# All eight u tiles of a hybrid encoder layer in seven products, with pairs of u and gates in turn

## The chip, the cores and the metric

The kernel runs on one core of a Trainium2 chip. The core has five engines with queues of their own: PE (TensorE, matmuls), DVE (VectorE), ACT (ScalarE), POOL (GpSimd) and SP (SyncE, which here issues the loads of weights). The metric is the device time of one execution in microseconds (us). The profile stores times in us from the start of the span unless marked ns.

## The reference

One layer of an encoder over 512 positions of width 1024, in float32. Cut to what matters here:

```python
x1 = x  + rmsnorm(W_out(sig(a_ret) * W_ret_o(Retention(h)) + sig(a_sgu) * W_sgu_o(SGU(h)))),  h = rmsnorm(x)
y  = x1 + rmsnorm(ConvGatedMLP(rmsnorm(x1)))

q, k, v, g, u, sv, a_ret, a_sgu = split(h @ w_in)       # 512, 512, then six of 1024 columns
y_ret = (layernorm(retention(q, k, v)) * silu(g)) @ w_ret_o
sv    = layernorm(gelu(sv)) in chunks of 128 positions, 4 groups of 256 columns
mixed = einsum('gpq,bnqgc->bnpgc', w_spatial, sv) + b_spatial
y_sgu = (gelu(u) * mixed) @ w_sgu_o
```

The change concerns u, the gate sig(a_ret), the output of the retention branch W_ret_o, and `mixed`.

## The kernel before, in words

Activations lie transposed: a tile has 128 features by 512 positions, and eight tiles make 1024 features. Every float32 operand is split into a high and a low part of the rounded type fp32r, and a product is three matmuls: high by high, high by low, low by high. A split is a copy on ACT (the high part, L97) and a subtraction on DVE (the low part, L116).

There are two ways to make output tiles. A *whole* tile (`f_block`) takes one weight block of 128x1024 and 8 x 3 = 24 matmuls of 512 columns. A *Pair* makes two output tiles at once, in seven products of half the width in place of eight (Strassen's way): 7 x 12 = 84 matmuls of 256 columns, with seven weight forms, four of which are sums (`w_form`, T1 to T4), and with ready sums of the activations. For the pairs of gates (`GATE0` to `UP0`) T2 and T4 are summed on POOL (L201, L204), for others on DVE. A Pair holds three PSUM banks, numbered 0 to 2, and has three parts:

- the first part: product into bank 0, which ACT copies to SBUF; product into bank 1, which DVE adds to it; product into bank 2; a fourth one that goes on adding in bank 0, behind the first copy, and is copied by ACT too
- the second: product with S3, again into bank 0, copied by ACT, and subtracted by DVE from bank 2
- the third: one more product into bank 0, behind that copy, and one into bank 2; DVE scales them by the row norm `rbc`, and ACT applies gelu or sigmoid.

The stage in question comes after the retention's own work and ends before the gates of the SGU branch. In order on PE, before: four whole u tiles (`UW = 4`), two u Pairs, then four times `gated_pair(ogh, ogl)`: a Pair of gates with two whole tiles of the retention's output between its parts (of which DVE multiplies the PSUM result by the gate, L1051), followed by two mixes `mix(2 * j)`, `mix(2 * j + 1)`, 16 small matmuls over positions, after which DVE forms mix and multiplies u by it and the result yh, yl is split for the SGU branch's product. The statistics and the norm of sv (`sv_stats`, `sv_scale`, `sv_norm`; L717 on ACT) hang behind the u tiles. After the stage four `gated_pair(yh, yl)` follow.

What sets the order: the code is recorded operation by operation, and a scheduler places the instructions of every engine in a queue; `tc.issue_after(x)` forces what follows behind x. Weights are asked for LOOK = 4 units ahead of use in the order of the list `units` (L111 on), are loaded by SP into four tiles `raw` (128x1024, 512 KB), split into nine slots, and wait there. A queue works off its instructions strictly in order, so a row that waits holds the rows behind it.

Of the kernel before, what the change touches and what calls it, by code (L numbers as in the profile page):

```python
# [15 lines left out]
P = 128  # L16
# [9 lines left out]
EPS = 1e-6  # L26
NW = 146
SV0, U0, GATE0, GATE1 = 24, 32, 40, 72
UW = 4
LOOK = 4  # L30
NBLK = 66
WARM = 17
# [17 lines left out]
def tile_block(ctx: ExitStack, tc, xT, x, wall, par, cs, wsp, bsp, gpost, gffn, out):  # L50
# [48 lines left out]
    def two(t):  # L99
        return t.rearrange("p (n c) -> p n c", n=2)  # L100
# [176 lines left out]
    def w_get(look=LOOK):  # L277
# [9 lines left out]
            n += w_size(u)  # L287
        return w_ready.pop(i)

    def mm3(o, ah, al, bh, bl, start, stop, skip=False):  # L290
        nc.tensor.matmul(o, ah, bh, start=start, stop=False, skip_group_check=skip)  # L291
        nc.tensor.matmul(o, ah, bl, start=False, stop=False, skip_group_check=skip)  # L292
        nc.tensor.matmul(o, al, bh, start=False, stop=stop, skip_group_check=skip)  # L293


    part = const("part", [P, NPAR])
# [603 lines left out]
    class Pair:  # L900
# [9 lines left out]
        def product(self, b, act, first, w=None):  # L910
            wh, wl = w or w_get()
            o = self.b[b][:, T0]
            for k in range(4):
                c = slice(k * P, (k + 1) * P)
                h_, l_ = act(k)
                for n, (w_, a_) in enumerate(((wh, h_), (wh, l_), (wl, h_))):
                    self.last = nc.tensor.matmul(  # L917
                        o, w_[:, c], a_, start=first and k == n == 0, stop=k == 3 and n == 2,
                        skip_group_check=True,
                    )  # L920
            return self.two(o)

        def x(self, first, t):
# [46 lines left out]

    bst = lo64("bst", F32)
    nc.gpsimd.dma_start(bst, bsp.rearrange("g p -> (g p)")[None, :].to_broadcast([P, S]))
    uT, late = [], None
    U_HOMES = [lambda: lo64("u", F32), lambda: hi192("u", F32)] + [lambda: blk(n="u")] * 2 + [lambda: hi192("u", F32)] * 4
    for j in range(UW):
        with tc.issue_after(summed) if j == 0 else ExitStack():
            o = f_block(xh, xl, KD)
        u = U_HOMES.pop()()
        i = v.tensor_mul(two(u), in_turn(o), two(rbc)).ins
        g = nc.scalar.activation(out=u, in_=u, func=AF.Gelu_apprx_tanh).ins  # L980
        uT.append(u)
        with tc.issue_after(i):
            sv_stats(((0, 1), (2, 3), (), ())[j])
        if j == 1:
            sv_scale()
        if j > 1:
            with tc.issue_after(g):
                sv_norm(j - 2, range((NT, 2)[j - 2]))
    for j in range(UW // 2, KD // 2):
        p = Pair(AF.Gelu_apprx_tanh, lambda: U_HOMES.pop()(), None, rbc)  # L990
        p.part1()
        if late:
            late.part3()
        p.part2()
        late = p
        uT += p.t
        if j == UW // 2:
            with tc.issue_after(p.copied):
                sv_norm(1, range(2, NT))
    yh, yl = [], []  # L1000

    def mix(j):
        gs = slice((j // 2) * P, (j // 2 + 1) * P)
        add = tmp("add", (P, P))
        v.scalar_tensor_tensor(
            out=add, in0=rws[:, gs], scalar=col(LNB + j), in1=bst[:, gs],
            op0=ALU.mult, op1=ALU.add,
        )
        o = ps()
        for t in range(NT):  # L1010
            nc.tensor.matmul(  # L1011
                o[:, t * P : (t + 1) * P],
                svz[t, j // 4][:, (j % 4) * P : (j % 4 + 1) * P],
                wst[:, gs],
                start=True,
                stop=True,
            )
        m = tmp("mix")
        v.scalar_tensor_tensor(
            out=m.rearrange("p (t q) -> p t q", t=NT),  # L1020
            in0=o.rearrange("p (t q) -> p t q", t=NT),
            scalar=col(LNG + j),
            in1=add[:, None, :].to_broadcast([P, NT, P]),
            op0=ALU.mult,
            op1=ALU.add,
        )
        v.tensor_mul(uT[j], m, uT[j])
# [6 lines left out]
    def gated_pair(ah, al, late=None):  # L1034

        p = Pair(AF.Sigmoid, lambda: tmp("sig"), None, rbc)
        with tc.issue_after(late.last.ins) if late else ExitStack():
            p.part1()
        if late:
            with tc.issue_after(p.last.ins):  # L1040
                late.part3()
# [5 lines left out]
    r = []  # L1047
    for j in range(KD // 2):
        for o, t in gated_pair(ogh, ogl, late if j == 0 else None):
            b = (lo64("r", F32) if j == 0 else hi192("r", F32) if j < 3 else blk(n="r"))  # L1050
            v.tensor_mul(two(b), in_turn(o), two(t))  # L1051
            r.append(b)
# [608 lines left out]
```

## Time and profile before

| | |
|---|---|
| median of three runs | 785.31 us (785.3 to 785.34) |
| profiled execution | 785.08 us |
| its span | 783.3 us |
| PE busy | 775.6 us, 99% |
| DVE busy | 626.5 us, 80% |
| ACT busy | 467.8 us, 60% |
| POOL busy | 104.0 us, 13% |
| granted clock of PE | 0.998 |

The span is what the profiler recorded from the first to the last instruction; the execution's time is 1.78 us more. Rows of a group give the line, the engine, the operation, output <- input by name, and times; the chain that ended last is followed back from the last instruction, at each step to what released it.

### The profile page before, as it was taken

The numbers are of one execution on the slowest core, as the hardware profiler recorded it, in microseconds if no ns is written. First come the engines' busy times: TensorE is split into PE (matmuls) and PEld (weight loads), VectorE is DVE, ScalarE is ACT, GpSimd is POOL, SyncE is SP. The second block draws the span as 40 slices with busy tenths as digits, with TensorE's granted clock in tenths as the row PEclk, the third lists the DMA queues.
The fourth block names the chain that finished last, engine by engine and source line by source line (L and its number), as shares of the span: only waits on it lengthen the run. The fifth ranks groups of instructions, "written<-read, shape, count | busy, mean of one in ns | idle before, by whom it ended". The sixth has DMA issues, their size and how long they took to land.

```text
span 783.3 us, 13258 instructions
## 1 busy us (share of the span) xinstructions
PE 775.6 (99%) x5067; PEld 720.3 (92%) x5067; DVE 626.5 (80%) x1067; ACT 467.8 (60%) x848; POOL 104.0 (13%) x132
## 2 busy tenths in 40 slices
PE   9999999999999999999999999999999999999996
PEld 8888998998899999999998998999999998999996
DVE  7467887788786877867765679989999889877987
ACT  7555558689385544444444776657777578644542
POOL 0040001130012111032211200001111012200001
PEclk9999999999999999999999999999999999999999
DMA  8782224453123333223459111425555365632244
GB/s 293 260 266 88 81 82 162 108 133 126 55 106 108 108 108 108 106 84 108 138 161 344 57 69 39 122 108 141 141 149 149 108 196 114 170 114 108 108 162 162
DMA packets 35889, 104.78 MB, mean 134 GB/s; under 512 B 4401, under 2 KB 6321, under 8 KB 35825
## 3 DMA queue, kind: packets, MB, share of 16 engines
q1 hardware_dynamic: 27936, 87.81, 31.8%
q0 software_dynamic: 7024, 14.95, 9.0%
q10 hardware_dynamic: 864, 1.18, 0.4%
q8 instruction: 39, 0.64, 0.3%
q14 instruction: 26, 0.20, 0.1%
HBM read 91.34 MB, written 4.19 MB: 122 GB/s over the span
## 4 chain that ended last, share of the span: by engine, by line
PE 98%; DVE 1%; ACT 0%; POOLq 0%; issue 0%; POOL 0%; DVEq 0%
PE ps L917 22%; PE ps L291 13%; PE ps L293 13%; PE ps L292 13%; PE ps L1354 11%; PE ps L746 5%; PE ps L625 4%; PE ps L627 4%; PE ps L626 4%; PE ps L1089 2%; PE ps L1091 2%; PE ps L1090 2%; PE ps L1370 2%; PE ps L1011 1%; PE ps L411 1%; PE ps L393 0%
## 5 line engine op out<-in xcount | busy, mean ns | idle before, releaser
L116 DVE TENSOR_TENSOR wl<-raw,wh 128x1024 fp32r<-128x1024 f32 (+1 forms) x88 | 100.6, 1152 | 56.1 <-issue 20.6
L97 ACT ACTIVATE wf<-raw 128x512 fp32r<-128x512 f32 x126 | 75.6, 624 | 83.8 <-PE ps L292 37.1
L97 ACT ACTIVATE wh<-raw 128x1024 fp32r<-128x1024 f32 (+2 forms) x92 | 89.1, 981 | 28.9 <-DMA raw<-wall 15.5
L917 PE MATMUL ps<-sh,wf 128*128 128x256 f32 x576 | 105.3, 275 | 0.0
L116 DVE TENSOR_TENSOR wf<-raw,wf 128x512 fp32r<-128x512 f32 x126 | 93.3, 754 | 14.9 <-ACT wf L97 14.7
L917 PEld LDWEIGHTS ps<-sh,wf 128*128 128x128 f32 x576 | 91.7, 192 | 0.8 <-ACT u L97 0.2
L291 PE MATMUL ps<-h2h,wh 128*128 128x512 f32 (+1 forms) x256 | 90.7, 354 | 0.0
L293 PE MATMUL ps<-h2h,wl 128*128 128x512 f32 (+1 forms) x256 | 90.4, 353 | 0.0
L292 PE MATMUL ps<-h2l,wh 128*128 128x512 f32 (+1 forms) x256 | 90.4, 353 | 0.0
L917 PE MATMUL ps<-sl,wf 128*128 128x256 f32 x288 | 79.3, 275 | 0.0
L1354 PE MATMUL ps<-dh,fh 128*128 128x256 f32 x216 | 59.5, 276 | 0.0
L1354 PE MATMUL ps<-dh,fl 128*128 128x256 f32 x216 | 59.5, 275 | 0.0
L1354 PE MATMUL ps<-dl,fh 128*128 128x256 f32 x216 | 59.4, 275 | 0.0
L917 PEld LDWEIGHTS ps<-sl,wf 128*128 128x128 f32 x288 | 55.3, 192 | 0.4
L97 ACT ACTIVATE dh<-raw 128x768 fp32r<-128x768 f32 (+1 forms) x36 | 33.6, 950 | 33.5 <-DVE raw L224 17.6
L293 PEld LDWEIGHTS ps<-h2h,wl 128*128 128x128 f32 x256 | 48.6, 190 | 5.1
L291 PEld LDWEIGHTS ps<-h2h,wh 128*128 128x128 f32 x256 | 48.7, 190 | 4.5
L292 PEld LDWEIGHTS ps<-h2l,wh 128*128 128x128 f32 x256 | 48.7, 190 | 4.4
L627 PE MATMUL ps<-wh,xl 128*128 128x512 f32 x128 | 48.6, 379 | 0.0
L626 PE MATMUL ps<-wl,xh 128*128 128x512 f32 x128 | 48.5, 379 | 0.0
L625 PE MATMUL ps<-wh,xh 128*128 128x512 f32 x128 | 48.5, 380 | 0.0
L917 PE MATMUL ps<-xh,wf 128*128 128x256 f32 x240 | 43.8, 276 | 0.0
(343 smaller groups left out, 2185.8 us busy)
## 6 DMA issues: line engine op xcount, KB each, us to landing
raw<-wall SPq DMA_DIRECT2D x144, 512.0 KB, 3.6
x<-x SPq DMA_DIRECT2D x24, 256.0 KB, 5.9
fl<-gp POOLq DMA_DIRECT2D x12, 256.0 KB, 4.0
swap<-qkraw POOLq DMA_DIRECT2D x16, 128.0 KB, 4.3
x<-x POOLq DMA_DIRECT2D x8, 256.0 KB, 2.3
fl<-fs POOLq DMA_DIRECT2D x8, 256.0 KB, 3.3
xT<-xT SPq DMA_DIRECT2D x7, 256.0 KB, 5.5
xT<-xT POOLq DMA_DIRECT2D x4, 256.0 KB, 4.0
```

The costliest lines, as they stand in the source:

```text
L97: return nc.scalar.activation(out=o, in_=i, func=AF.Copy)
L116: low[0] = nc.vector.tensor_sub(lo, src, as32(hi)).ins
L291: nc.tensor.matmul(o, ah, bh, start=start, stop=False, skip_group_check=skip)
L292: nc.tensor.matmul(o, ah, bl, start=False, stop=False, skip_group_check=skip)
L293: nc.tensor.matmul(o, al, bh, start=False, stop=stop, skip_group_check=skip)
L625: nc.tensor.matmul(acc[t], xh[k][:, c], turns(wh[:, f]), start=k == 0, stop=False)
L626: nc.tensor.matmul(acc[t], xh[k][:, c], turns(wl[:, f]), start=False, stop=False)
L627: part_end[0] = nc.tensor.matmul(acc[t], xl[k][:, c], turns(wh[:, f]), start=False, stop=k == KD - 1)
L746: nc.tensor.matmul(bank[t], a_[:, c], turns(w_[:, f]), start=first and k == i == 0, stop=last and k == 3 and i == 2, skip_group_check=True,)
L917: self.last = nc.tensor.matmul(o, w_[:, c], a_, start=first and k == n == 0, stop=k == 3 and n == 2, skip_group_check=True,)
L1089: nc.tensor.matmul(o, ah, turns(bh), start=k == 0, stop=False)
L1354: nc.tensor.matmul(o, a_[:, c], turns(w_[:, f]), start=j == t == i == 0, stop=j == DP - 1 and i == 2 and n not in (M2, M3, M4), skip_group ...
```

## The change

All eight u tiles become four Pairs; the whole u tiles are gone. The loop order of the stage is replaced by a table, `MIDDLE`, of 40 steps. A step's name has a kind and a number: `W5` is whole tile 5 of the retention's output, `M0` mix 0; `U10` is part 1 of u Pair 0, `U21` part 2 of u Pair 1, `G33` part 3 of gate Pair 3. Each step is recorded behind PE's last matmul of the step before it. u Pairs and gate Pairs come in turn, and W and M steps stand between them. `units`, the order in which weights are loaded and split, follows the same table. A gate is now ready after its whole tiles rather than before: ACT copies a whole tile from PSUM to r, and DVE multiplies r by the gate in SBUF when the gate's third part is done. The statistics and the norm of sv hang behind W0 to W4. The SGU branch's `gated_pair(yh, yl)` keeps its order.

```diff
-UW = 4
+MIDDLE = [(i[:-1], int(i[-1])) for i in (
+    "W0 W1 U10 W2 U20 G10 U30 G20 U11 G30 W3 M0 M1 U21 G11 U31 G21 U12 G31 M2 M3 W4 U22 G12 U32 W5 G22 U13 G32"
+    " W6 W7 M4 M5 U23 G13 U33 M6 G23 M7 G33"
+).split()]
...
-        elif U0 + UW <= i < GATE0:
-            units += pair
-            i += 2
+        elif i == U0:
+            us, gs = ([[(f, k + n * m) for f in FORMS] for n in range(KD // 2)] for k, m in ((U0, 2), (GATE0, 4)))
+            ws = [("blk", GATE0 + 4 * (n // 2) + 2 + n % 2) for n in range(KD)]
+            for what, n in MIDDLE:
+                units += {"W": lambda: ws[n : n + 1], "U1": lambda: us[n][:4], "U2": lambda: us[n][4:],
+                          "G1": lambda: gs[n][:4], "G2": lambda: gs[n][4:]}.get(what, list)()
+            i = GATE0 + 2 * KD
...
-    for j in range(UW):
-        with tc.issue_after(summed) if j == 0 else ExitStack():
-            o = f_block(xh, xl, KD)
-        u = U_HOMES.pop()()
-        i = v.tensor_mul(two(u), in_turn(o), two(rbc)).ins
-        g = nc.scalar.activation(out=u, in_=u, func=AF.Gelu_apprx_tanh).ins
...
-    for j in range(UW // 2, KD // 2):
-        p = Pair(AF.Gelu_apprx_tanh, lambda: U_HOMES.pop()(), None, rbc)
-        p.part1()
-        if late:
-            late.part3()
-        p.part2()
-        late = p
...
-        for o, t in gated_pair(ogh, ogl, late if j == 0 else None):
-            v.tensor_mul(two(b), in_turn(o), two(t))
-        mix(2 * j)
-        mix(2 * j + 1)
+    def whole(n):
+        o = f_block(ogh, ogl, KD)
+        r.append(lo64("r", F32) if n < 3 else hi192("r", F32) if n == 3 else blk(n="r"))
+        done = copy(two(r[n]), in_turn(o)).ins
+        if n < 2:
+            with tc.issue_after(low[0]):
+                sv_stats(((0, 1), (2, 3))[n])
+                if n:
+                    sv_scale()
+        if 0 < n < 5:
+            with tc.issue_after(done):
+                sv_norm((n - 1) // 2, range(NT)[:2] if n % 2 else range(NT)[2:])
+
+    def u_first(n):
+        us[n] = Pair(AF.Gelu_apprx_tanh, lambda: hi192("u", F32), None, rbc)
+        us[n].part1()
+
+    def u_third(n):
+        us[n].part3()
+        uT[2 * n], uT[2 * n + 1] = us[n].t
+
+    def g_first(n):
+        gs[n] = Pair(AF.Sigmoid, lambda: tmp("sig"), None, rbc)
+        gs[n].part1()
+
+    def g_third(n):
+        gs[n].part3()
+        for i, t in enumerate(gs[n].t):
+            v.tensor_mul(r[2 * n + i], r[2 * n + i], t)
...
+    pe_last[0] = summed
+    for what, n in MIDDLE:
+        with tc.issue_after(pe_last[0]):
+            does[what](n)
```

In the rows that follow, `wf` and `wh` are split weights of a form and of a whole block, `raw` the loaded ones, `sig` a gate tile, `ps` a PSUM bank, `yh` and `yl` the split product of u and mix; the line numbers of the changed kernel differ (L97 and L116 became L100 and L119, L198, L199 became L205, L206, the Pair's lines L938 to L968 became L948 to L978, L717 became L726).

ACT in the first part of a gate Pair of the kernel before, the one behind mixes 0 and 1; `sig_2861<-ps_2863` is the copy that the Pair's fourth product waits for:

```order
L97 ACTIVATE wh_2897<-raw_2895 128x1024
L97 ACTIVATE yh_2843<-u_2242 128x512
L97 ACTIVATE sig_2861<-ps_2863 128x256
L97 ACTIVATE yh_2857<-u_2286 128x512
L97 ACTIVATE wf_2917<-raw_2913 128x512
```

ACT at the step G12 of the changed kernel (first part of gate Pair 2), behind mixes 2 and 3 and W4; `sig_3087<-ps_3089` is that copy:

```order
L100 ACTIVATE yh_3010<-u_2567 128x512
L100 ACTIVATE yh_3024<-u_2568 128x512
L100 ACTIVATE wh_3062<-raw_3060 128x1024
L100 ACTIVATE r_3056<-ps_3031 128x512
L726 ACTIVATE sv_1912<-sv_1912,sshift,srstd 128x512
L726 ACTIVATE sv_1913<-sv_1913,sshift,srstd 128x512
L100 ACTIVATE u_2893<-ps_2894 128x256
L100 ACTIVATE wf_3080<-raw_2913 128x512
L100 ACTIVATE wf_3084<-raw_2948 128x512
L100 ACTIVATE sig_3087<-ps_3089 128x256
```

Between the second yh and the copy stood nothing (the copy was ahead of it); now wh, r, two tiles of sv, a u copy and two wf stand there.

DVE during the last gate Pair of the stage, around the sums of weights that are formed there, before:

```order
L116 TENSOR_TENSOR wf_3365<-raw_3361,wf_3365 128x512
L947 TENSOR_TENSOR sig_3309<-sig_3309,rbc_567 128x256
L198 TENSOR_TENSOR raw_3385<-raw_3361 128x512
L1005 SCALAR_TENSOR_TENSOR add_3505<-rws_1911,part,bst_2205 128x128
L116 TENSOR_TENSOR wf_3382<-raw_3362,wf_3382 128x512
L199 TENSOR_TENSOR raw_3361<-raw_3361,raw_3362 128x512
L116 TENSOR_TENSOR wf_3389<-raw_3385,wf_3389 128x512
L116 TENSOR_TENSOR wf_3417<-raw_3385,wf_3417 128x512
```

DVE of the changed kernel from the T1 sum (L205) of the weights that are formed around G13, U33 and M6, to the scaled second tile of u Pair 3 (L977), on which ACT's last gelu waits:

```order
L205 TENSOR_TENSOR raw_3501<-raw_3473 128x512
L948 TENSOR_TENSOR sig_3480<-ps_3483,sig_3480 128x256
L206 TENSOR_TENSOR raw_3473<-raw_3473,raw_3474 128x512
L119 TENSOR_TENSOR wf_3505<-raw_3501,wf_3505 128x512
L119 TENSOR_TENSOR wf_3521<-raw_3501,wf_3521 128x512
L957 TENSOR_TENSOR sig_3480<-sig_3480,rbc_567 128x256
L972 TENSOR_TENSOR u_3249<-ps_3251,rbc_567 128x256
L989 SCALAR_TENSOR_TENSOR add_3579<-rws_1911,part,bst_2213 128x128
L975 TENSOR_TENSOR u_3250<-ps_3253,u_3250 128x256
L119 TENSOR_TENSOR wl_3596<-raw_3593,wh_3595 128x1024
L977 TENSOR_TENSOR u_3250<-u_3250,rbc_567 128x512
```

The sums of weights stand now among the closing rows of a u Pair, and L977 comes behind a full-width subtraction.

ACT before, at the second part of a gate Pair (the first of the SGU branch's, right behind the stage); the second `sig_3534<-ps_3535` is the copy that the first product of its third part waits for:

```order
L97 ACTIVATE sig_3534<-ps_3535 128x256
L97 ACTIVATE wf_3606<-raw_3586 128x512
L97 ACTIVATE wf_3613<-raw_3609 128x512
L97 ACTIVATE wf_3641<-raw_3609 128x512
L97 ACTIVATE sig_3534<-ps_3535 128x256
```

The same place at G23 of the changed kernel, with G33 waiting for `sig_3481<-ps_3482`:

```order
L100 ACTIVATE wf_3521<-raw_3501 128x512
L100 ACTIVATE wh_3595<-raw_3593 128x1024
L973 ACT_TABLE_LOAD
L973 ACTIVATE u_3249<-u_3249 128x512
L978 ACTIVATE u_3250<-u_3250 128x512
L100 ACTIVATE sig_3481<-ps_3482 128x256
```

The copy stood behind splits of weights; now a table load and both gelus of u Pair 3 are ahead of it.

More of the change, by code (lines that the diff above doesn't have):

```diff
@@ L292, in mm3 @@
         nc.tensor.matmul(o, ah, bl, start=False, stop=False, skip_group_check=skip)
-        nc.tensor.matmul(o, al, bh, start=False, stop=stop, skip_group_check=skip)
+        pe_last[0] = nc.tensor.matmul(o, al, bh, start=False, stop=stop, skip_group_check=skip).ins
     part = const("part", [P, NPAR])
@@ L920, in product @@
                     )
+            pe_last[0] = self.last.ins
             return self.two(o)
@@ L972, in tile_block @@
     nc.gpsimd.dma_start(bst, bsp.rearrange("g p -> (g p)")[None, :].to_broadcast([P, S]))
-    uT, late = [], None
-    U_HOMES = [lambda: lo64("u", F32), lambda: hi192("u", F32)] + [lambda: blk(n="u")] * 2 + [lambda: hi192("u", F32)] * 4
-    for j in range(UW):
-        with tc.issue_after(summed) if j == 0 else ExitStack():
-            o = f_block(xh, xl, KD)
-        u = U_HOMES.pop()()
-        i = v.tensor_mul(two(u), in_turn(o), two(rbc)).ins
-        g = nc.scalar.activation(out=u, in_=u, func=AF.Gelu_apprx_tanh).ins
[L981 to L988, printed above, removed]
-    for j in range(UW // 2, KD // 2):
-        p = Pair(AF.Gelu_apprx_tanh, lambda: U_HOMES.pop()(), None, rbc)
-        p.part1()
-        if late:
-            late.part3()
-        p.part2()
-        late = p
[L996 to L999, printed above, removed]
+    uT = {}
     yh, yl = [], []
@@ L1010, in mix @@
         for t in range(NT):
-            nc.tensor.matmul(
+            pe_last[0] = nc.tensor.matmul(
                 o[:, t * P : (t + 1) * P],
@@ L1016, in mix @@
                 stop=True,
-            )
+            ).ins
         m = tmp("mix")
@@ L1031, in mix, with gated_pair @@
         yl.append(l_)
-    def gated_pair(ah, al, late=None):
+    def gated_pair(ah, al):
         p = Pair(AF.Sigmoid, lambda: tmp("sig"), None, rbc)
[L1037 to L1041, printed above, removed]
+        p.part1()
         o = [f_block(ah, al, KD)]
@@ L1045, in gated_pair @@
         return zip(o, p.t)
-    r = []
-    for j in range(KD // 2):
-        for o, t in gated_pair(ogh, ogl, late if j == 0 else None):
-            b = (lo64("r", F32) if j == 0 else hi192("r", F32) if j < 3 else blk(n="r"))
-            v.tensor_mul(two(b), in_turn(o), two(t))
-            r.append(b)
-        mix(2 * j)
-        mix(2 * j + 1)
+    r, us, gs = [], {}, {}
+    def whole(n):
[23 more added lines that the diff above has]
+            v.tensor_mul(r[2 * n + i], r[2 * n + i], t)
+    does = {
+        "W": whole, "M": mix, "U1": u_first, "U2": lambda n: us[n].part2(), "U3": u_third,
+        "G1": g_first, "G2": lambda n: gs[n].part2(), "G3": g_third,
+    }
+    pe_last[0] = summed
+    for what, n in MIDDLE:
+        with tc.issue_after(pe_last[0]):
+            does[what](n)
     mh, ml = [], []
```

3 lines of the change are left out of this document (2 added, 1 removed).

## The prediction

> **What bounds the kernel now.** I read the page first, then the chain of work for the stage that is rewritten, then the groups of VectorE (DVE) and ScalarE (ACT) by line, then timelines of single places. From the page, the span, TensorE's (PE's) busy time and the chain that ended last; then two stretches, whose columns are length, PE, weight loads, DVE, ACT, POOL (busy us and count), granted clock, DMA share and GB/s:
>
> ```profile
> span 783.3 us, 13258 instructions
> PE 775.6 (99%) x5067; PEld 720.3 (92%) x5067; DVE 626.5 (80%) x1067; ACT 467.8 (60%) x848; POOL 104.0 (13%) x132
> ...
> PE 98%; DVE 1%; ACT 0%; POOLq 0%; issue 0%; POOL 0%; DVEq 0%
> ```
>
> ```profile
> 220.20:260.80 40.60, 40.57 (x319) 39.11 (x318) 30.67 (x50) 26.07 (x45) 5.96 (x4) 1.00 0.29 103
> 260.80:336.50 75.70, 75.70 (x524) 71.24 (x523) 58.58 (x98) 32.64 (x57) 12.19 (x7) 1.00 0.28 99
> ```
>
> PE is the bound, at the granted clock 1.00. The time falls by what PE no longer computes and rises by every wait that PE is given. DVE is busy 58.58 of 75.70 us, so a PE order that needs results sooner can make DVE and ACT late. The chain prices PE's work (start, length, what, count):
>
> ```profile
> 199.04 0.46 PE ps L839 x2
> 199.51 0.22 PE ps L291
> ...
> 220.23 5.80 PE ps L917 x52
> 226.06 18.58 PE ps L917 x164
> 244.63 0.22 PE ps L291
> ...
> 249.82 1.34 PE ps L917 x12
> ...
> 253.75 2.68 PE ps L917 x24
> ...
> 259.02 1.78 PE ps L1011 x16
> ```
>
> ```profile
> 260.80 5.36 PE ps L917 x48
> ```
>
> A matmul of 256 columns takes 5.36/48 = 0.1117 us. The four whole u tiles are 96 matmuls of 512 columns from 199.51 to 220.23, 20.72 us, or 5.18 a tile. So the steps of the new table cost: W 5.18, first part 5.36, second 1.34, third 2.68, M 1.78/2 = 0.89.
>
> **What the change removes.** Two whole tiles are 10.36 us; a pair in seven products is 84 x 0.1117 = 9.38. Two such exchanges save 2 x 0.98 = 1.96 us of PE, all on the path. The two pairs of before stand in the chain from 220.23 to 244.63, 24.40 us, for 216 products = 24.12: there PE waits 0.28 us (near 226). That place is gone, so another 0.28 goes: -2.24 together.
>
> **What it adds.** Retention tiles (W) are copied by ACT into r, and DVE multiplies r in SBUF afterwards: eight 512-column copies on ACT. The two new pairs bring six copies of 256 columns to ACT, eight rows more to DVE, and for each pair seven half-width weight splits and four sums of weights in place of two full-width splits. The table alternates gelu and sigmoid, so ACT loads its function table seven times in the stage instead of once. By the rows below, that is 6 x 0.37 + 8 x 0.59 + 14 x 0.62 - 4 x 1.05 + 6 x 1.28 = 19 us more for ACT and, with 2 x 2.8 - 4 x 0.69 for the pairs' own rows and 22 x 0.68 - 4 x 1.22 for the weights, 13 us more for DVE in a stage of about 126 us. POOL's rows and the number of weight loads on the SP queue are unchanged. PE hides all this as long as no copy is late for the PSUM bank that a product must reuse: in each Pair, product four and the first product of the third part write into bank 0 again, after ACT's copy of it. So I summed each queue row by row from 199.34, where PE starts the stage, with these rows (minimum/median/maximum ns; what is named by L numbers at the places A and B below are lines of the changed kernel, 3 to 10 above their counterparts here):
>
> ```profile
> 199.34 0.38 PE L291 MATMUL ps<-xh,wh 128*128 128x512 f32 x1
> ```
>
> ```profile
> L116 DVE TENSOR_TENSOR wf<-raw,wf x54: 673/684/1739, 200.9 to 343.8; 128x512 fp32r<-128x512 f32 x54
> ...
> L116 DVE TENSOR_TENSOR wl<-raw,wh x13: 1216/1224/1534, 196.3 to 341.3; 128x1024 fp32r<-128x1024 f32 x13
> L97 ACT ACTIVATE wf<-raw x54: 610/624/643, 200.2 to 342.6; 128x512 fp32r<-128x512 f32 x54
> L97 ACT ACTIVATE sig<-ps x15: 362/383/388, 238.9 to 337.3; 128x256 f32<-128x256 f32 x15
> L97 ACT ACTIVATE wh<-raw x12: 1048/1050/1077, 196.5 to 337.6; 128x1024 fp32r<-128x1024 f32 x12
> L97 ACT ACTIVATE rws<-ps x1: 589/589/589, 199.7 to 199.7; 128x512 f32<-128x512 f32 x1
> L717 ACT ACTIVATE sv<-sv,sshift,srstd x8: 797/798/815, 216.6 to 227.4; 128x512 f32<-128x512 f32 x8
> ```
>
> ```profile
> 260.93 0.74 DVE L1019 SCALAR_TENSOR_TENSOR mix<-ps,part,add 128x512 f32<-128x512 f32 x1
> 261.59 0.34 DVE L1005 SCALAR_TENSOR_TENSOR add<-rws,part,bst 128x128 f32<-128x128 f32 x1
> 261.85 0.68 DVE L1027 TENSOR_TENSOR u<-mix,u 128x512 f32<-128x512 f32 x1
> 262.45 0.74 DVE L1019 SCALAR_TENSOR_TENSOR mix<-ps,part,add 128x512 f32<-128x512 f32 x1
> ```
>
> A DVE row starts 0.08 us before the one ahead of it ends (0.74 takes 0.66 of the queue, 0.68 takes 0.60, 0.42 takes 0.34). On ACT it is 0.10, by the next fence: 0.63 takes 0.54 (258.46 to 259.00).
>
> ```profile
> 256.52 0.63 ACT L97 ACTIVATE wf<-raw 128x512 fp32r<-128x512 f32 x1 [4.00 <-PE ps L917]
> 257.17 1.28 ACT L963 ACT_TABLE_LOAD   x1
> 258.46 0.63 ACT L963 ACTIVATE sig<-sig 128x512 f32<-128x512 f32 x1
> 259.00 0.61 ACT L968 ACTIVATE sig<-sig 128x512 f32<-128x512 f32 x1
> ```
>
> A table load costs ACT 1.28 us, and the sigmoid starts 0.01 us after it. [...]
>
> One more price, DVE against POOL:
>
> ```profile
> 230.35 0.68 DVE L199 TENSOR_TENSOR raw<-raw,raw 128x512 f32<-128x512 f32 x1
> 230.98 1.74 DVE L116 TENSOR_TENSOR wf<-raw,wf 128x512 fp32r<-128x512 f32 x1
> 232.65 0.41 DVE L938 TENSOR_TENSOR u<-ps,u 128x256 f32<-128x256 f32 x1
> ```
>
> ```profile
> 230.45 1.72 POOL L201 TENSOR_TENSOR raw<-raw,raw 128x512 f32<-128x512 f32 x1 [14.01 <-DVE wf L116]
> 234.80 1.28 POOL L204 TENSOR_TENSOR raw<-raw,raw 128x512 f32<-128x512 f32 x1 [2.63 <-DVE wf L116]
> ```
>
> While POOL forms the T2 sum (to 232.17), a DVE row that reads two SBUF tiles is held to the sum's end and half a microsecond beyond: 1.74 instead of 0.68, 1.06 lost. The gate pairs' T2 and T4 are formed on POOL.
>
> **Place A, the first part of gate pair 2.** Ahead of it stand five W, five first, five second, four third parts and four M: 25.90 + 26.80 + 6.70 + 10.72 + 3.56 = 73.68, so it starts at 273.02, and its fourth product is due three products (4.02) later, at 277.04. It waits for ACT's copy of the first product. Backwards: u pair 1's last product ends on PE at 255.34; DVE reaches the row that follows it (L972) at 256.05, then 0.34 + 0.34 + 1.14 + 0.69 bring the scaled u to 258.56; ACT's gelu and the next wf copy end at 259.75; DVE's wf subtraction at 260.47 gives a raw tile back, and SP loads the next weights, which land after
>
> ```profile
> raw<-wall SPq DMA_DIRECT2D x144, 512.0 KB, 3.6
> ```
>
> at 264.1. From there DVE has fifteen rows up to u times mix of M3: nine of 0.60, two of 0.66, two of 0.34, one of 0.26 and the last in full, 0.69: 8.4 us, and 272.5 if nothing is held. POOL's T2 starts right behind the first of them and holds the wf row (1.0), T4 meets the last (0.4): 273.9. On ACT then come yh, wh, r, two sv, the u copy, two wf and the copy in question: 0.53 + 0.95 + 0.50 + 1.40 + 0.28 + 1.06 + 0.38 = 5.1, to 279.0, or 279.1 with PE's own start: PE waits 2.1 us (0.8 unheld). The load has a bound above: in the crowded stretch 232 to 262 its median was
>
> ```profile
> raw<-wall SPq DMA_DIRECT2D x7, 512.0 KB, 4.2
> ```
>
> which makes 2.7. I take 2.1, since the load here is one of two, as most of the 144 are.
>
> **Place B, the third part of gate pair 3.** Let T be the end of u pair 3's second part. Until its first product PE has 5.36 + 2.68 + 0.89 + 1.34 + 0.89 = 11.16. That product waits for ACT's copy of the S3 product of the same gate pair (1.34 + 0.89 = 2.23 before), which stands in ACT's queue behind a 1.05 copy of wh, a table load and two gelus, the second of which waits for DVE's L977. On DVE the mix of M4 (PE done at T - 2.23) and the rows behind it up to the T1 sum take 0.66 + 0.26 + 0.60 + 0.66 + 0.34 + seven of 0.60 and 0.69 = 7.4; with 0.3 until the mix starts that is T + 5.5. Then 0.34, T3, two wf, L957, L972, add, L975, wl and L977 take 0.34 + 0.60 + 1.20 + 0.34 + 0.34 + 0.26 + 0.34 + 1.14 + 0.69 = 5.25, with 0.2 to 0.5 of waiting for ACT's copies: T + 11.0. POOL's T2 holds T3 (0.6) and T4 holds L957 (1.2): T + 12.8. Gelu and copy add 0.53 + 0.38, PE's start 0.05: T + 13.8, a wait of 2.6 (1.1 unheld, with the longer wait for the copies). I take 2.6, because both sums start while DVE has rows with two SBUF inputs next in line.
>
> The first pair of the SGU gates waits 0.15 for its copy by the same sum. The tightest places that still hold, the fourth products of u pairs 1 and 2 (due about 235 and 260.7), have 0.2 to 0.3 us left, and late loads would open them for up to 0.5 each.
>
> **Sum.** -1.96 - 0.28 + 2.1 + 2.6 + 0.15 = +2.6 us. The profiled execution took 785.08, so 787.7; it stands 0.23 under the median of the runs, so against 785.31 the forecast is 787.9, 0.33% slower. 0.2%, 1.57 us, is about what a measurement of this kernel tells from no change: under 783.74 is faster, over 786.88 slower.
>
> **Rivals.**
> - POOL's sums fall between DVE rows instead of onto them (in before, T4 at 234.80 holds nothing). Then A is 0.8 and B 1.1: -2.24 + 0.8 + 1.1 + 0.15 = -0.2, or 785.1, the same. Against it: both places have DVE rows back to back when the sums start.
> - ACT is never late, the other side. The price is A and B themselves: the fourth product at A is met if u times mix of M3 is done by 271.9 (277.04 - 5.1), and B if L977 ends by T + 10.2 (11.16 - 0.91 - 0.05). For it speaks that ACT is busy only 32.64 of 75.70 us now, and that shortening waits elsewhere in the queue (a copy 0.3 us sooner, each 0.1 us in a load) counts fully at A. Then 785.31 - 2.24 = 783.1, faster. It decides where the two waits together stay under 0.65 us.
> - The loads take 4.2 as in the crowded stretch: A 2.7, B 2.6 to 3.2, and 0.3 to 0.5 at each of the two tight places: 785.31 - 2.24 + 6.05 to 7.05, or 789.1 to 790.1.
> [...]
>
> **How the numbers follow.** Both waits with POOL's hold: 0.57, own range 786.7 to 789.2. Unheld: 0.21. Never late: 0.11. Slow loads: 0.07. Drains: 0.04. The predicted time is the likeliest case's, 787.9. The range takes in the unheld case below and slow loads above: 785.0 to 790.5. Faster 0.12: the case of no late copy and 0.01 of the unheld one. Same 0.22: the rest of that, 0.20, and 0.02 of the first that ends under 786.88. Slower 0.66: what is left.
>
> **What the new profile would show.** If right: in the chain, PE's products no longer run through; a gap of about 2 us ahead of the fourth product of gate pair 2, released by ACT's sig copy at L100, and one of 2 to 3 us ahead of the third part of gate pair 3, released by the same line; the L119 and L957 rows there last 1.3 to 1.7 us with POOL's L208 and L211 beside them; seven table loads of 1.28. PE's busy time is down by 2.0. If PE shows no wait over 0.5 us in the stage, the sums down the queues are wrong; if the gaps are there but DVE's rows are not stretched, only the hold is. Waits at other places would mean the weights' loads, whose order changed, arrive later than 3.6.

## The result and the profile after

| | before | after |
|---|---|---|
| median of the timed executions | 785.3 us (784.55 to 785.45, 6) | 790.15 us (788.53 to 791.43, 6) |
| ratio | | 1.0063, 95% interval 1.0053 to 1.0073 |
| profiled execution | 785.08 us | 791.16 us |
| its span | 783.3 us | 789.4 us |

The changed kernel is slower, by 4.85 us between the medians; 2.6 was forecast. Its page, the span, the busy times and the chain that ended last:

```profile
span 789.4 us, 13477 instructions
...
PE 777.0 (98%) x5139; PEld 723.3 (92%) x5139; DVE 640.8 (81%) x1093; ACT 484.4 (61%) x878; POOL 102.4 (13%) x132
...
PE 92%; DVE 4%; ACT 1%; issue 1%; DMA 0%; POOLq 0%; POOL 0%; DVEq 0%; SPq 0%; ACTq 0%
```

PE, which held 98% of the chain, holds 92% now. What DVE and ACT have gained there is the length of the rows that led up to PE's waits, not the waits themselves, which are far shorter. PE's busy time should have fallen by 2.0 us and rose by 1.4 instead. PE's waits in the stage, from its timeline (start, length, line, what, and in brackets the idle time before it and who ended it):

```profile
261.18 0.38 PE L926 MATMUL ps<-sh,wf 128*128 128x256 f32 x1 [0.22 <-ACT u L100]
...
279.85 0.38 PE L926 MATMUL ps<-sh,wf 128*128 128x256 f32 x1 [2.05 <-ACT sig L100]
...
327.07 0.38 PE L926 MATMUL ps<-xh,wf 128*128 128x256 f32 x1 [2.10 <-ACT sig L100]
```

These are the fourth product of u pair 2, place A and place B, each behind the ACT copy that was named. An idle of 2.05 costs PE 2.32: the step between two starts of matmuls grows from 0.11 to 2.33 (277.52 to 279.85), and the one behind it from 0.11 to 0.21. What stands behind the two long waits is seen in windows of 2 us (length, PE, weight loads, DVE, ACT, POOL, granted clock, DMA share, GB/s):

```profile
278.00:280.00 2.00, 0.15 (x1) 0.16 (x2) 1.39 (x3) 2.00 (x6) 0.00 (x0) 1.00 0.65 240
280.00:282.00 2.00, 2.00 (x11) 2.00 (x12) 2.00 (x5) 0.94 (x2) 0.00 (x0) 0.55 0.68 227
282.00:284.00 2.00, 2.00 (x13) 2.00 (x12) 1.16 (x3) 0.38 (x1) 0.00 (x0) 0.60 0.77 264
284.00:286.00 2.00, 2.00 (x18) 1.97 (x18) 1.82 (x4) 1.36 (x3) 0.00 (x0) 1.00 0.14 55
...
326.00:328.00 2.00, 0.93 (x8) 0.93 (x9) 2.00 (x6) 1.78 (x4) 0.00 (x0) 0.99 0.67 240
328.00:330.00 2.00, 2.00 (x12) 2.00 (x11) 1.85 (x4) 0.90 (x2) 0.00 (x0) 0.50 0.29 94
330.00:332.00 2.00, 2.00 (x14) 2.00 (x13) 1.91 (x4) 0.26 (x1) 0.00 (x0) 0.65 0.73 248
332.00:334.00 2.00, 2.00 (x20) 2.00 (x20) 1.18 (x3) 1.98 (x3) 0.00 (x0) 1.00 0.55 207
```

The granted clock falls to a half just after PE resumes, twice, for 3.41 us each (280.19 to 283.60 and 327.98 to 331.39). A busy window of 2 us then holds 11 to 14 matmuls in place of 18 to 20. From the start of U22 (272.27) to the end of U32 (285.60) PE took 13.33 us for 84 products, in place of 84 x 0.1117 = 9.38, and so lost 3.95: 2.32 of waiting and 1.6 by the clock. At B it is about the same, 2.35 and 1.6 (the 60 products behind that wait take 8.43 us in place of 6.70; 0.1 of the difference belongs to the wait).

The chain to A, from the timelines of DVE, POOL and ACT:

```profile
264.73 0.69 DVE L206 TENSOR_TENSOR raw<-raw,raw 128x512 f32<-128x512 f32 x1 [0.59 <-DMA raw<-wall]
265.38 1.72 DVE L119 TENSOR_TENSOR wf<-raw,wf 128x512 fp32r<-128x512 f32 x1
...
273.72 0.99 DVE L1011 TENSOR_TENSOR u<-mix,u 128x512 f32<-128x512 f32 x1
```

```profile
264.80 1.76 POOL L208 TENSOR_TENSOR raw<-raw,raw 128x512 f32<-128x512 f32 x1 [19.00 <-DMA raw<-wall]
272.57 1.59 POOL L211 TENSOR_TENSOR raw<-raw,raw 128x512 f32<-128x512 f32 x1 [6.01 <-DVE wf L119]
```

```profile
274.75 0.63 ACT L100 ACTIVATE yh<-u 128x512 fp32r<-128x512 f32 x1 [2.52 <-DVE u L1011]
275.28 1.04 ACT L100 ACTIVATE wh<-raw 128x1024 fp32r<-128x1024 f32 x1
276.23 0.58 ACT L100 ACTIVATE r<-ps 128x512 f32<-128x512 f32 x1
276.71 1.51 ACT L726 ACTIVATE sv<-sv,sshift,srstd 128x512 f32<-128x512 f32 x2
278.12 0.37 ACT L100 ACTIVATE u<-ps 128x256 f32<-128x256 f32 x1
278.38 1.14 ACT L100 ACTIVATE wf<-raw 128x512 fp32r<-128x512 f32 x2
279.42 0.37 ACT L100 ACTIVATE sig<-ps 128x256 f32<-128x256 f32 x1
```

The load ends DVE's wait at 264.7, POOL's T2 stretches the wf row to 1.72 and T4 the last row to 0.99, ACT sits idle for 2.52 us until u times mix of M3 is there, and then works through nine rows without a gap until the copy ends at 279.79. The chain to B, on DVE, POOL's two sums beside it, and ACT's end of it:

```profile
319.49 1.70 DVE L206 TENSOR_TENSOR raw<-raw,raw 128x512 f32<-128x512 f32 x1
...
322.99 1.03 DVE L989 SCALAR_TENSOR_TENSOR add<-rws,part,bst 128x128 f32<-128x128 f32 x1
```

```profile
319.37 1.28 POOL L208 TENSOR_TENSOR raw<-raw,raw 128x512 f32<-128x512 f32 x1 [9.40 <-DVE raw L205]
322.48 1.39 POOL L211 TENSOR_TENSOR raw<-raw,raw 128x512 f32<-128x512 f32 x1 [1.83 <-DVE wf L119]
```

```profile
322.27 1.28 ACT L973 ACT_TABLE_LOAD   x1
323.56 0.63 ACT L973 ACTIVATE u<-u 128x512 f32<-128x512 f32 x1
326.12 0.63 ACT L978 ACTIVATE u<-u 128x512 f32<-128x512 f32 x1 [1.93 <-DVE u L977]
326.66 0.36 ACT L100 ACTIVATE sig<-ps 128x256 f32<-128x256 f32 x1
```

L206 and the small add row, 0.69 and 0.34 when nothing holds them, last 1.70 and 1.03 beside POOL's sums. The table load is done 2.6 us before the second gelu can start; that one waits for DVE's L977.

### The profile page after: what moved, and what is told of

It reads as the page before. It is cut to its first block, busy times and chain, and to the rows that moved or that the text cites. A ratio compares the mean times of both kernels' runs of the same rounds, so it can differ in the third digit from the quotient of the medians.

```text
span 789.4 us, 13477 instructions
## 1 busy us (share of the span) xinstructions
PE 777.0 (98%) x5139; PEld 723.3 (92%) x5139; DVE 640.8 (81%) x1093; ACT 484.4 (61%) x878; POOL 102.4 (13%) x132
## 4 chain that ended last, share of the span: by engine, by line
PE 92%; DVE 4%; ACT 1%; issue 1%; DMA 0%; POOLq 0%; POOL 0%; DVEq 0%; SPq 0%; ACTq 0%
PE ps L926 21%; PE ps L300 12%; PE ps L301 12%; PE ps L302 12%; PE ps L1366 11%; PE ps L755 5%; PE ps L634 4%; PE ps L636 4%; PE ps L635 3%; PE ps L1101 2%; PE ps L1103 2%; PE ps L1102 2%; PE ps L1382 2%; DVE wf L119 1%; PE ps L420 1%
## 5 line engine op out<-in xcount | busy, mean ns | idle before, releaser
L119 DVE TENSOR_TENSOR wl<-raw,wh 128x1024 fp32r<-128x1024 f32 (+1 forms) x84 | 95.3, 1143 | 52.9 <-issue 15.9
L100 ACT ACTIVATE wf<-raw 128x512 fp32r<-128x512 f32 x140 | 84.9, 624 | 70.7 <-issue 21.0
L926 PE MATMUL ps<-sh,wf 128*128 128x256 f32 x640 | 120.0, 279 | 2.3 <-ACT sig L100 2.1
L119 DVE TENSOR_TENSOR wf<-raw,wf 128x512 fp32r<-128x512 f32 x140 | 105.7, 768 | 13.0 <-ACT wf L100 12.4
L926 PEld LDWEIGHTS ps<-sh,wf 128*128 128x128 f32 x640 | 103.8, 195 | 3.3 <-ACT sig L100 2.2
L100 ACT ACTIVATE wh<-raw 128x1024 fp32r<-128x1024 f32 (+2 forms) x88 | 84.8, 977 | 30.0 <-DMA raw<-wall 18.2
L926 PE MATMUL ps<-sl,wf 128*128 128x256 f32 x320 | 89.0, 278 | 0.0
L926 PEld LDWEIGHTS ps<-sl,wf 128*128 128x128 f32 x320 | 62.4, 195 | 0.4
L926 PE MATMUL ps<-xh,wf 128*128 128x256 f32 x288 | 53.4, 279 | 2.1 <-ACT sig L100 2.1
L100 ACT ACTIVATE dh<-raw 128x768 fp32r<-128x768 f32 (+1 forms) x36 | 33.6, 951 | 32.5 <-DVE raw L231 16.6
L926 PEld LDWEIGHTS ps<-xh,wf 128*128 128x128 f32 x288 | 46.6, 196 | 2.5 <-ACT sig L100 2.3
```

The source lines that it names most:

```text
L100: return nc.scalar.activation(out=o, in_=i, func=AF.Copy)
L119: low[0] = nc.vector.tensor_sub(lo, src, as32(hi)).ins
L926: self.last = nc.tensor.matmul(o, w_[:, c], a_, start=first and k == n == 0, stop=k == 3 and n == 2, skip_group_check=True,)
```

## The experiments

My theory: the two waits come from DVE's queue, lengthened by POOL's sums, and from what stands in ACT's queue behind it; where a wait is long the clock falls too and adds some 1.6 us. Rivals: the table loads, the loads of weights, and DVE's load as such, whatever the order. The loads of weights were not tried by an experiment, but the trace of the changed kernel speaks against them: their median from issue to landing in the stage, 199 to 336, is 3.5 us, as before, and the one that ends DVE's wait ahead of A was issued at 261.09 and was there at 264.7.

**What stands in ACT's queue at A.** The last two norms of sv hang behind W5:

```diff
-        if 0 < n < 5:
+        if n in (1, 2, 3, 5):
             with tc.issue_after(done):
-                sv_norm((n - 1) // 2, range(NT)[:2] if n % 2 else range(NT)[2:])
+                sv_norm(n // 3, range(NT)[:2] if n % 2 and n < 5 else range(NT)[2:])
```

> The last two norms of sv (two ACT rows, 1.4 us of ACT's queue) hang behind W5 in place of W4, and so no longer stand ahead of the sig copy that PE waits for at place A. Theory (ACT's queue behind u times mix of M3 sets the wait at A): the wait at A falls from 2.05 to about 0.7, the granted clock stays at 1.00 there, B keeps its wait of about 2.1; the time is 1.4 us lower for the wait and about as much again where the clock fell at A: 787 to 788.2. Rival (a load or a weight split ends last at A): the wait stays near 2 us, 789.5 to 790.5.

Measured: 788.14 us, ratio 1.0032 (1.0020 to 1.0044), within the range. PE's waits at A and B:

```profile
278.32 0.38 PE L926 MATMUL ps<-sh,wf 128*128 128x256 f32 x1 [0.62 <-ACT sig L100]
...
324.21 0.58 PE L926 MATMUL ps<-xh,wf 128*128 128x256 f32 x1 [2.39 <-ACT sig L100]
```

A falls by the 1.4 us of the two rows, and the clock stays at 1.00 there; B keeps its wait and the fall behind it (0.56 and 0.59 in the two windows from 324). So ACT's queue sets the wait at A, row by row.

**More of PE's work ahead of B.**

```diff
-    " W6 W7 M4 M5 U23 G13 U33 M6 G23 M7 G33"
+    " W6 M4 M5 U23 G13 U33 M6 G23 M7 W7 G33"
```

> The step W7 is moved from ahead of M4 to between M7 and G33, so PE has 5.18 us more work between the S3 product of gate pair 3 and the product that waits for its copy. Theory: the wait at B (2.1) and the fall of the clock behind it go, A stays as it is: 786.5 to 788. Rival (DVE is behind altogether at the end of the stage, and the wait only moves to the first SGU gate pair): a wait of 1 us or more appears there, and the time stays at 789 or above.

Measured: 786.32 us, ratio 1.0017 (1.0007 to 1.0027), just below the range. B is gone, and A is there as before; a part moves on to the first SGU gate pair:

```profile
279.67 0.38 PE L926 MATMUL ps<-sh,wf 128*128 128x256 f32 x1 [1.88 <-ACT sig L100]
...
330.40 0.38 PE L926 MATMUL ps<-sh,wf 128*128 128x256 f32 x1 [0.53 <-ACT sig L100]
```

In this profiled execution the clock stayed at 1.00 behind the idle of 1.88.

**Both moves.**

> Both moves together. Theory: A is 0.7, B is gone, the clock is 1.00 throughout the stage, the tight place at u pair 2 keeps 0.2: 785.3 - 2.2 + 0.7 + 0.2 + 0.15 = 784.1, between 783.5 and 785. Rival (the rows of DVE moved between are the limit): 786 or above with waits at new places.

Measured: 785.44 us, ratio 1.0001 (0.9992 to 1.0010), 0.4 over the range. A is 0.51 and B is gone, but the first SGU gate pair waits more than its 0.15:

```profile
278.62 0.38 PE L926 MATMUL ps<-sh,wf 128*128 128x256 f32 x1 [0.51 <-ACT sig L100]
...
329.73 0.38 PE L926 MATMUL ps<-sh,wf 128*128 128x256 f32 x1 [0.92 <-ACT sig L100]
```

Two of the changed kernel's waits are replaced by small ones, and what is left about equals the saved products.

**POOL's sums.** In the stage's gate pairs:

```diff
+            if GATE0 <= i < GATE1:
+                w_raw["T2"], w_raw["T4"] = w_raw["B22"], w_raw["B21"]
+            else:
                 eng.tensor_tensor(out=w_raw["T2"], ...)
```

(the sum for T4 is left out in the same way)

> The sums T2 and T4 of the gate pairs of the rewritten stage are left out (the forms take B22 and B21 in their place, the same splits and products follow), so POOL does nothing there and cannot hold DVE. Theory: the held rows at A (1.72 and 0.99 in place of 0.68) and at B (1.70, 1.03) take their 0.68 and 0.34; A falls from 2.05 to 0.8 and B from 2.1 to about 0.7, no fall of the clock: 785.3 - 2.2 + 0.8 + 0.7 + 0.2 = 784.8, at most 786. Rival (POOL's sums only fill time in which DVE waits anyway): both waits stay above 1.7, 788.5 to 790.

Measured: 784.17 us, ratio 0.9983 (0.9974 to 0.9993); idle 0.52 at A and 0.39 at B, clock 1.00.

```profile
277.46 0.38 PE L930 MATMUL ps<-sh,wf 128*128 128x256 f32 x1 [0.52 <-ACT sig L100]
...
321.35 0.38 PE L930 MATMUL ps<-xh,wf 128*128 128x256 f32 x1 [0.39 <-ACT sig L100]
```

Without POOL's sums 1.5 and 1.7 us of the two waits go. (The range of the edit takes in the SGU branch's four gate pairs too, where PE waits for none of this: sixteen sums are left out, eight of them in the stage.) This leaves two readings: POOL's hold, or that the forms are ready sooner without the sums. The trace of the changed kernel speaks for the hold: from 199 to 340 a split waited for POOL's sum once, 0.43 us (ACT, until 320.68), and the second gelu behind it still had to wait 1.93 us for DVE. The sums on DVE, below, take away the hold and leave the sums.

**The table loads.**

```diff
-        gs[n] = Pair(AF.Sigmoid, lambda: tmp("sig"), None, rbc)
+        gs[n] = Pair(AF.Gelu_apprx_tanh, lambda: tmp("sig"), None, rbc)
```

> The gates of the rewritten stage take gelu in place of the sigmoid (that leaves out the gates' own function), so ACT's function table is not changed within the stage; all else as in the changed kernel. Theory (the table loads run while ACT would wait for DVE anyway: at B the second gelu waits for L977 1.9 us after the load's end): the wait at A falls by 0.7 at most, B stays within 0.3 of 2.1: 788.3 to 790.2. Rival (each of the loads lies in a chain): 1.28 off both waits, and no fall of the clock: 785.5 to 787.

Measured: 791.33 us, ratio 1.0070 (1.0055 to 1.0086), above both ranges. Without a single load in the stage B is as it was, and A is longer:

```profile
280.30 0.38 PE L926 MATMUL ps<-sh,wf 128*128 128x256 f32 x1 [2.82 <-ACT sig L100]
...
327.53 0.38 PE L926 MATMUL ps<-xh,wf 128*128 128x256 f32 x1 [2.10 <-ACT sig L100]
```

So taking the loads away shortens neither wait, and the rival falls: in the changed kernel ACT stands idle for DVE behind them, 2.52 us ahead of A and 1.93 ahead of B. Of the 0.77 by which A grew, about 0.3 is PE coming there sooner (its wait begins at 277.48, not 277.79), and 0.45 is u times mix of M3, done at 275.16 in place of 274.71; some rows of DVE and ACT stand in another order in this kernel.

**The seven products without the interleaving.** In the kernel before:

```diff
-UW = 4
+UW = 0
...
     for j in range(UW // 2, KD // 2):
         p = Pair(AF.Gelu_apprx_tanh, lambda: U_HOMES.pop()(), None, rbc)
-        p.part1()
+        with tc.issue_after(summed) if j == 0 else ExitStack():
+            p.part1()
...
+        with tc.issue_after(p.copied):
+            if j < 2:
+                sv_stats(((0, 1), (2, 3))[j])
+            if j == 1:
+                sv_scale()
+            if j > 1:
+                sv_norm(j - 2)
```

> The kernel before with all eight u tiles as four Pairs in a row, in its own order of steps: the seven products without the interleaving. Theory (DVE has 9.0 us of rows a u pair, beside 9.38 of products, and the statistics of sv besides): PE waits inside the u pairs, about 2 us in the third pair, 0.9 at the first gate pair and 0.3 in the second pair: 785.3 - 2.0 + 3.3 + 0.2 = 786.8. Rival (the saved products come out whole): 783.3.

Measured: 786.22 us, ratio 1.0014 (1.0004 to 1.0023).

```profile
231.86 0.38 PE L917 MATMUL ps<-sh,wf 128*128 128x256 f32 x1 [2.06 <-ACT u L97]
...
242.12 0.38 PE L917 MATMUL ps<-sh,wf 128*128 128x256 f32 x1 [0.62 <-ACT sig L97]
```

Four u pairs in a row, with the statistics of sv, ask for more of DVE than PE's time for them leaves: DVE is busy 42.78 of the 44 us from 196 to 240. The saved products are eaten by these two waits: in this order, too, the gain went into the queues of DVE and ACT.

**The clock.** In the kernel with both moves, W4's copy r is made six times (long), or three times (short) in place of once:

```diff
         done = copy(two(r[n]), in_turn(o)).ins
+        for _ in range(5 if n == 4 else 0):
+            done = copy(two(r[n]), in_turn(o)).ins
```

> The kernel with both moves (785.44, idle 0.51 at A, clock 1.00) with ACT's copy r of W4 made six times in place of once, which adds 5 x 0.50 us ahead of the copy that PE waits for at A. Theory (a gap above about 2 us halves the granted clock for about 3.5 us): idle 3.0 at A, then the clock at 0.5 for some 3.5 us in every execution, so 2.5 + 1.8 us more: 789.7, mean clock 0.996. Rival (the fall of the clock at A and B in the changed kernel has nothing to do with the gaps' length): 2.5 us more, 787.9, mean clock 0.998 or above.

> As the long gap, but with W4's copy r made three times, 2 x 0.50 us more ahead of the copy at A: an idle of about 1.5 us. Theory (the clock falls only behind an idle of about 2 us or more): the clock stays at 1.00 behind A and in the mean of every execution (0.997 to 0.999), 785.4 + 1.0 = 786.4. Rival (any idle of a microsecond or more can bring the clock down): a mean clock of 0.996 or below in some executions and a median above 787.

Measured: 790.87 us, ratio 1.0070 (1.0055 to 1.0086), for the long one, with an idle of 3.58 at A and the clock at 0.52 and 0.62 in the windows from 282 on; its mean clock was 0.993 to 0.995 in all four executions. The time is 1.2 over the forecast, of which 0.6 is the longer idle (3.0 was expected). And 786.55 us, ratio 1.0014 (1.0002 to 1.0026), for the short one; its profiled execution shows an idle of 1.60 with the clock at 1.00, but two executions of ten had a mean clock of 0.995, and they are the two longest (788.12 and 787.54).

```profile
281.21 0.38 PE L926 MATMUL ps<-sh,wf 128*128 128x256 f32 x1 [3.58 <-ACT sig L100]
```

```profile
282.00:284.00 2.00, 2.00 (x12) 2.00 (x11) 0.71 (x3) 0.06 (x1) 0.00 (x0) 0.52 0.78 248
```

```profile
279.74 0.38 PE L926 MATMUL ps<-sh,wf 128*128 128x256 f32 x1 [1.60 <-ACT sig L100]
```

So the gap causes the fall: the long one, put into a kernel without falls, brought it, and by the mean clocks it did so in every execution. Its length alone does not say whether it comes (the idle of 2.05 at A in the changed kernel was followed by a fall, that of 2.06 in the pairs in the old order was not), and my expectation of the short one was too sharp.

**The mixes earlier.** On top of both moves:

```diff
-    ... M0 M1 U21 G11 U31 G21 U12 G31 M2 M3 W4 U22 G12 ...
+    ... M0 M1 U21 G11 U31 M2 G21 M3 U12 G31 W4 U22 G12 ...
```

> The kernel with both moves, and M2 and M3 spread before and behind the second part of gate pair 1 (U31 M2 G21 M3 U12 G31), two to three steps earlier. DVE has u times mix of M3 done sooner, while PE's cover up to the fourth product at G12 is the same sum of steps from there on. Theory: the wait at A is 0, as is B; left are the tight places at u pair 2 (0.2 to 0.5 with the restart), and the first SGU gate pair (0.9): 785.3 - 2.2 + 0.4 + 1.0 = 784.5 or below, to 783.5. Rival (DVE's sum of rows to that point is the limit, whatever their order): a wait of 0.5 or more moves to a product of u pair 2 or gate pair 1, and the time stays at 785.4.

Measured: 784.87 us, ratio 0.9990 (0.9981 to 0.9998), 0.4 over the range. A is gone, but the rival has a part in it: 0.45 at the fourth product of gate pair 1, and 1.06 at the first SGU gate pair.

```profile
251.72 0.38 PE L926 MATMUL ps<-sh,wf 128*128 128x256 f32 x1 [0.45 <-ACT sig L100]
...
328.70 0.38 PE L926 MATMUL ps<-sh,wf 128*128 128x256 f32 x1 [1.06 <-ACT sig L100]
```

**The sums on DVE.** The same edit at both sums, in the changed kernel, in the last one, and in the kernel before:

```diff
-            eng = nc.vector if i < GATE0 or i >= UP0 else nc.gpsimd
+            eng = nc.vector if i < GATE1 or i >= UP0 else nc.gpsimd
```

> The changed kernel with the sums T2 and T4 of the stage's gate pairs formed by DVE in place of POOL: eight rows of 0.60 more on DVE, which is the engine that is late, and nothing on POOL that holds it. Theory (a POOL sum costs DVE a hold of 0.4 to 1.2 us where it meets rows of two SBUF inputs, so DVE is better off doing it itself): idle at A about 1.3 in place of 2.05, at B 0.2 to 0.5 in place of 2.1, clock 1.00: 785.3 - 2.2 + 2.8 + 0.5 = 786.4. Rival (the holds fall into time in which DVE waits anyway, and work added to DVE makes it later): A and B at 2.2 or above, 790 to 791.5.

> The kernel with both moves and M2, M3 spread (784.87; idle 0.45 at the fourth product of gate pair 1, 1.06 at that of the first SGU gate pair) with the stage's T2 and T4 on DVE. Theory: the held rows ahead of both places (1.71, 1.77, 1.78) take 0.69, the idle of 0.45 goes and that of 1.06 falls to 0.5 or below: 785.2 - 2.2 + 0.7 = 783.6, between 783.0 and 784.3. Rival (DVE, with 4.8 us more, is the limit there): both waits stay, 784.8 or above.

> The kernel before with the stage's T2 and T4 on DVE in place of POOL, and nothing else: whether the gain of the last kernel is that of the sums alone. Theory (PE waits nowhere in the stage of the kernel before but for 0.28 us, which is in the u pairs, whose sums DVE forms already): 785.3, within 0.6. Rival (POOL's holds cost the kernel before as well): 784 or below.

Measured, in this order: 785.18 us, ratio 1.0000 (0.9991 to 1.0009); 782.81 us, ratio 0.9967 (0.9955 to 0.9979); 785.16 us, ratio 0.9996 (0.9987 to 1.0006). This edit, too, reaches the SGU branch's gate pairs, eight sums beside the stage's eight. The first is 1.2 under its forecast, the second 0.2 under its range, the third as forecast. In the changed kernel the waits shrink to 1.03 and 0.27 though DVE has eight rows more to do in the stage:

```profile
278.10 0.38 PE L926 MATMUL ps<-sh,wf 128*128 128x256 f32 x1 [1.03 <-ACT sig L100]
321.87 0.38 PE L926 MATMUL ps<-xh,wf 128*128 128x256 f32 x1 [0.27 <-ACT sig L100]
```

The wf subtractions, in the changed kernel and with the sums on DVE (count, minimum/median/maximum ns; the rows from 199 to 340, which takes in the first SGU gate pair, where the 1770 is; the longest of the stage itself is the 1.72 at A):

```profile
L119 DVE TENSOR_TENSOR wf<-raw,wf x62: 636/682/1770, 198.4 to 338.1; 128x512 fp32r<-128x512 f32 x62
```

```profile
L119 DVE TENSOR_TENSOR wf<-raw,wf x65: 641/684/697, 198.3 to 337.0; 128x512 fp32r<-128x512 f32 x65
```

That is POOL's hold, and the rival of DVE's load falls: more work on DVE, less of it late. The wait at A ends 1.75 us sooner, and half of that comes from further back. The sums of gate pair 1, some 35 us ahead of A, stretched two wf rows to 1.71 and 1.58 in the changed kernel; without that hold DVE begins the first mix of that place at 245.35 in place of 246.27, and the load ahead of A is issued at 260.18 in place of 261.09. With both moves and the earlier mixes no wait of PE is left in the stage; the window from 199 to 336, of this kernel:

```profile
199.00:336.00 137.00, 137.00 (x1020) 131.00 (x1020) 118.77 (x213) 87.66 (x149) 1.96 (x3) 1.00 0.30 101
```

It beats both kernels, the one before by 2.6 us between the medians of runs side by side (785.39 before). The sums alone do nothing for the kernel before, where PE waited for none of them.

## Why the prediction was right, and where it was off

- **The number**: slower was right, and for the reason given, waits at A and B. But 790.15 lies outside the range of that case alone (786.7 to 789.2). The stated range of 785.0 to 790.5 holds it because it took in slow loads too, and these did not come: that the time fell inside is luck.
- **What the change removes** was 2.24 us. The kernel with both moves, the earlier mixes and the sums on DVE has the change's pairs and no wait in the stage. From PE's first matmul of the stage to the first one behind the SGU gate pairs it takes 202.58 us, against 204.84 before: 2.26 less. By the medians it is 2.6 us faster, with an interval of 1.6 to 3.5 by its ratio. The term holds.
- **Place A** was put at 2.1 and measured an idle of 2.05, which cost 2.32. The steps stand as they were written: L977's end 259.15 (258.56 forecast), the load's end at 264.7 (264.1), a wf row of 1.72 under T2, the last row stretched by 0.3 under T4, u times mix of M3 at 274.7 (273.9), the copy's end at 279.8 (279.0). Each is late by 0.6 to 0.8, and so was the wait's end; PE came there 0.6 later than forecast as well, having lost 0.7 in and before u pair 2. The two delays cancel, which is luck. What the chain lacked is the hold by gate pair 1's sums, further back: it was begun at L972, put at 256.05; DVE came to that row at 256.68, and at 255.77 with the sums on DVE.
- **Place B** was put at 2.6 and was 2.10 idle, 2.35 in all. T was at 313.56 in this trace and L977 ended at T + 12.5 (T + 12.8). T2 held L206 by 1.0 in place of 0.6; T4 met the small add row (1.03, a hold of 0.7 in place of 1.2) and not L957.
- **The tight places** were given 0.2 to 0.3 us to spare; u pair 2's fourth product waited 0.22, and with the matmuls around it about 0.5. The first SGU gate pair, put at 0.15, did not wait.
- **The sum** of these, with the 0.7 that PE lost ahead of A, is -2.24 + 2.32 + 2.35 + 0.7 = 3.1 in place of 2.6. In the one execution whose mean clock was 0.999 the changed kernel took 788.53, 3.2 over the median of before.
- **The step that failed** is the price of a wait: a wait was counted at its own length, with PE at full speed behind it. The 1.6 us by the halved clock, at A and again at B, were left out: 3.1 + 3.2 = 6.3. Between the two matmuls named above the profiled execution took 211.23 us, 6.4 more than before, and as a whole it is 6.1 longer. By their mean clocks two of the six executions had both falls, three had one and one had none, and the median is 4.85 longer. Nothing in the stage of before shows this price, since PE waits there at most 0.3 us and the granted clock is 1.00.
- **The rival of the slow loads**: its time, 789.1 to 790.1, is nearest to the measured one, but what it says did not happen. The loads landed after 3.5 us in the median, in the stretch from 232 to 262 too, where 4.2 was feared. The drains, which were given 0.04, stand for a price of a table load beyond its own 1.28 us; no run shows that term. Seven table loads of 1.28 are in the changed kernel's stage. Behind five of them gelu or the sigmoid starts 0.01 to 0.03 us after the load's end (322.27 + 1.28 to 323.56 ahead of B), behind the other two ACT stands idle 0.30 us for DVE, and without the loads the waits remain (2.82 and 2.10). Even another 1.9 us behind the load would not have lengthened the wait at B, since ACT then stood idle 1.93 us for L977.
- The rival in which ACT is never late, and the one without POOL's hold, both failed as the sum said; the second became true by taking the sums off POOL: 785.18 measured, 785.1 worked out. That close a match is luck, since the waits left there are 1.03 and 0.27 where 0.8 and 1.1 were worked out.
- **What the change adds** in work was put at 13 us for DVE and 19 for ACT; the busy times on the two profile pages grew by 14.3 and 16.6.

## What to carry to other kernels

Where PE is the bound at 99%, price an order of steps by what every PSUM bank is waiting for, and carry the queues of DVE and ACT row by row to that copy; sums of busy time said nothing here. A wait of PE that gets near 2 us can cost more than itself: in the changed kernel the idles of 2.05 and 2.10 cost another 1.6 us each by the clock, while five kernels with idles of at most 1.06 show no sign of a fall in 47 executions. By these numbers two waits of 1 us are better than one of 2. A helper engine whose work stretches the rows of a late one (here a wf subtraction from 0.68 to 1.72 us) can be worth less than nothing: giving POOL's sums to the late DVE was worth 5 us, about 2.9 of it in shorter waits at A and B and most of the rest, by the mean clocks, in falls of the clock that no longer came.

## What the runs showed of the hardware

The granted clock. Kernels of these runs, by the longest idle of PE in the stage in the profiled execution, and how many of their executions had a mean granted clock of 0.996 or below (the 84 executions of the kernel before that were timed beside them had 0.997 to 0.999). Only the profiled execution shows its idle times and its falls; in the others the mean clock is a sign, and a rough one, since one fall changes it by no more than it scatters:

| longest idle, us | kernel | clock fell behind it in the profile | executions at 0.996 or below |
|---|---|---|---|
| up to 1.06 | both moves, no POOL sums, mixes early, sums on DVE, mixes early with sums on DVE | no | 0 of 47 |
| 1.60 | short gap | no | 2 of 10 |
| 1.88 | W7 late | no | 2 of 10 |
| 2.06 | pairs in the old order | no | 2 of 10 |
| 2.10 (and 2.05) | changed kernel | yes, both | 5 of 6 |
| 2.39 | sv behind W5 | yes | 4 of 7 |
| 2.82 (and 2.10) | no table switch | yes, both | 4 of 4 |
| 3.58 | long gap | yes | 4 of 4 |

In the changed kernel a fall lasted 3.41 us, from 0.34 and 0.91 us after PE had resumed (280.19 to 283.60 behind 279.85, 327.98 to 331.39 behind 327.07), and cost some 1.6 us of PE's work, which is a mean clock lower by about 0.002. Its six executions lie in that order: 791.16 and 791.43 at 0.993, 789.55 to 790.18 at 0.995 to 0.996, 788.53 at 0.999.

The length of the idle alone does not decide. The one of 2.05 at A was followed by a fall; the one of 2.06 in the pairs in the old order was not, with the clock at 1.00 in every window of 2 us from 228 to 236. In the short gap's profile an idle of 1.60 has no fall behind it, and two of its ten executions still have a mean clock of 0.995. What else decides was not tried by an experiment, so for a wait of about 2 us these runs do not say whether the 1.6 us come on top.

A long wait of PE cost about 0.27 us more than its idle time shows: at A the two steps around it took 2.33 and 0.21 in place of 0.11 each, 2.32 in all for 2.05 of idle.
